# Key pages of a paged decode: products and sums by halves of a page in every stage outside the attentions

## The chip, the cores and the metric

The kernel is one launch on one core of a Trainium2 chip. The core has five engines that run beside each other, each through its own list of instructions in a fixed order: TensorE (PE, matrix products; PEld is its loading of weights), VectorE (DVE), ScalarE (ACT), GpSimd (POOL) and SyncE (SP). An instruction waits on semaphores until what it reads has been written and what it overwrites has been read; what stands behind it on the same engine waits with it. SP, ACT and POOL also issue the DMA transfers. The metric is the time of one execution on the device in microseconds (us); of several executions the median counts.

## The reference

One step of a decoder layer for two groups that share the weights: a prompt of 1024 rows and a sample group of 8 sequences with one new row each. Everything is float32. Cut to what matters here:

```python
def fox_sample(q, k, v, logf, k_pool, v_pool, logf_pool, page_table):      # the 8 samples
    k_all = concatenate([k_pool[page_table].reshape(B, past, H, hd), k])   # past = 64 pages x 128 keys
    v_all = concatenate([v_pool[page_table].reshape(B, past, H, hd), v])
    c = cumsum(concatenate([logf_pool[page_table]..., logf]))
    return fox_attend(q, k_all, v_all, c[:, past:], c, qpos, kpos)

def fox_attend(q, k, v, cq, ck, qpos, kpos):
    s = einsum('bqhd,bkhd->bhqk', q, k) * 64 ** -0.5 + (cq - ck)           # then causal mask
    return einsum('bhqk,bkhd->bqhd', softmax(s), v)

# prompt: input projection -> attention (8 heads of 64) and spatial gating -> output projection
#         -> cross-attention into 256 memory rows (4 heads of 256)
#         -> MLP: up to 2 x 2816 columns, causal convolution of width 3, silu(gate) * val, down
# sample: the same layers, with fox_sample in place of the prompt's attention
```

For each of the 8 samples the scores `s` need 8192 cached keys of 8 heads x 64 numbers, gathered through the page table, multiplied with the sample's query and summed over the 64 numbers of each head.

## The kernel before

**The prompt (main work).** `prompt()` runs it in stages, named in `phase[0]`: `p1` (RMSNorm statistics and the input projection in column blocks Q, F, K, V, Z), `att0` and `att1` (the attention of rows 0 to 511 and 512 to 1023), then for each half of the rows `mid0`/`mid1` (output projection and cross-attention) and `ffn0`/`ffn1` (the MLP). The matrix products take float32 operands split in a high and a low part: `wload` loads a weight tile `wr`, ACT writes the high part `wh` (line 235), DVE the low part `wl` (line 236, `wr - wh`), and `gemm3` issues three products for each pair (lines 272, 273, 274). There are 4 buffers for `wl`. In the MLP, DVE also reads each up-projected tile out of PSUM for the convolution (lines 1299, 1300) and adds the down-projection to the residual (line 1332).

**The samples (background work).** `decode()` reads the cache. The 8192 keys of a sample are spread over the 128 partitions; one *page* below is a tile `kv` of 128 x 2048 numbers (1 MB): 4 keys of 512 numbers in each partition. There are 16 such pages of keys and 16 of values for each sample, 128 and 128 in all. `kstep(b, ch, st)` handles one page of keys: POOL gathers it (line 1420), DVE multiplies it in place with the query `qb` (line 1436), and sums each head's 64 products into the scores `s` (line 1440). After a sample's 16 pages come its softmax (`soft_max`, `soft_all`, `soft_exp`), and then `vstep`: POOL gathers a page of values (line 1482), and PE multiplies it by the weights in 4 narrow products (line 1488), 16 for a pair of pages. Keys and values share a ring of 4 `kv` buffers: POOL can gather the next page only when DVE has summed a page of keys, or PE has read a page of values. When all samples are through, `sample_rest()` takes them through the other layers.

**How a page of keys is cut.** In `att0`/`attx`/`att1` a page is done by quarters (lines 1427 and 1428, not touched here). Elsewhere the number of pieces is `sp`:

```python
sp = KS if phase[0][:3] == "mid" or held[0] else 1     # KS = 2
m = 4 // sp
```

With `sp = 1` the page is one product and one sum (the stages `p1` and `ffn0`). With `sp = 2` (`mid0`, `mid1`) there is a loop over the two products and behind it a loop over the two sums.

**What sets the order.** The main loop advances the background by a step whenever enough of the main work has been written (`PACE`). `kstep` writes under `behind(ENG.DVE)`, so that its instructions come behind what DVE has been given of the main work. The order written is not the order that runs: a scheduler places all instructions of each engine in a list, with a model of how long each one takes, and picks on each engine what is ready by that model. The lists of all engines are fixed when the program is built. A change of one instruction's size can thus move others.

## Time and profile before

| | |
|---|---|
| median of 3 runs | 1792.09 us (1789.83 to 1795.09) |
| the profiled execution | 1796.66 us, its span 1794.9 us |
| PE busy | 1736.6 us, 97% of the span |
| DVE busy | 1399.3 us, 78% |
| ACT busy | 734.4 us, 41% |
| POOL busy | 496.1 us, 28% |
| mean granted TensorE clock | 0.992 |
| DMA | 521.07 MB, mean 290 GB/s |

How to read the views. Times are in us from the start of the span unless marked ns. A row of instructions gives start and duration, engine, line, operation, `out<-in` by the program's tile names, and the shape; "x2" are two in a row, with the time from the first one's start to the last one's end; in brackets stands the idle time of the engine ahead of it and what ended it. The view by stages gives for each stretch of time how long each engine was busy, with the number of instructions in brackets, the granted clock, and the DMA engines' share and rate. Durations of neighbours on an engine can overlap by a little, so that the distance from start to start is the time that an instruction takes from the engine. A row of the waits says which engine and line waited for which, the total, how often, and the longest.

By the first rows of lines 236, 272 and 1332 of each stage, the stages lie about here: `p1` 0 to 260, the attentions 260 to 495, `mid0` 495 to 712, `ffn0` 712 to 1130, `mid1` 1130 to 1345, `ffn1` 1345 to 1780.

### The profile page before, as it was taken

To read this page: it belongs to the slowest core of one execution; us is meant where nothing else is said; L and a number is where in the kernel's file an instruction comes from. 1 tells how busy PE (TensorE), PEld (TensorE's weight loads), DVE (VectorE), ACT (ScalarE), POOL (GpSimd) and SP (SyncE) were. 2 spreads that over 40 slices of the span, in tenths; PEclk is the share of its full clock that TensorE was granted. 3 is DMA by queue.
4 is the path that set the end of the run, shared out by engine and by line. 5 is a ranking of instruction groups with operands and counts; after the bars stand their busy time and mean duration, and the time that the engine had idled before them with its cause. 6 is when DMAs were issued, how large, how long until landed. Compare 5 with 4: busy or idle time off the path is not lost.

```text
span 1794.9 us, 25099 instructions
## 1 busy us (share of the span) xinstructions
PE 1736.6 (97%) x9637; PEld 1286.9 (72%) x9637; DVE 1399.3 (78%) x1733; ACT 734.4 (41%) x1374; POOL 496.1 (28%) x461
## 2 busy tenths in 40 slices
PE   8999999889999999999999999999999999999997
PEld 5887777655677667777777777776676778767875
DVE  4689658988788987999999999887885549855344
ACT  6332256466643635333333244335353233333332
POOL 1252334432222332233322223333322122102110
PEclk9999999999999999999999999999999999999999
DMA  8886888787697975779788878978879687568982
GB/s 299 304 295 222 301 324 318 260 274 230 254 401 279 366 300 222 287 289 349 293 304 311 289 309 318 382 292 331 312 288 343 221 301 250 192 259 299 358 311 81
DMA packets 157075, 521.07 MB, mean 290 GB/s; under 512 B 20874, under 2 KB 40842, under 8 KB 124186
## 3 DMA queue, kind: packets, MB, share of 16 engines
q0 software_dynamic: 57168, 341.14, 50.2%
q1 hardware_dynamic: 92874, 165.73, 26.6%
q10 hardware_dynamic: 6912, 12.59, 1.9%
q8 instruction: 76, 1.25, 0.3%
q14 instruction: 45, 0.37, 0.1%
HBM read 495.47 MB, written 23.93 MB: 289 GB/s over the span
## 4 chain that ended last, share of the span: by engine, by line
PE 53%; DMA 9%; issue 8%; DVE 6%; POOL 2%; ACT 2%; POOLq 0%; DVEq 0%; ACTq 0%; SPq 0%
DMA kv<-cache_v,io 7%; PE ba L272 6%; PE ba L274 6%; PE ba L273 6%; PE dv L1488 4%; PE bb L272 3%; PE bb L273 3%; PE bb L274 3%; PE ba L1065 1%; PE ba L1064 1%; PE ba L1066 1%; PE dv L331 1%; DVE kv L1436 1%; PE dv L1764 1%; DVE s L1440 1%
## 5 line engine op out<-in xcount | busy, mean ns | idle before, releaser
L235 ACT ACTIVATE wh<-wr 128x1024 fp32r<-128x1024 f32 (+2 forms) x220 | 228.7, 1044 | 438.9 <-PE ba L273 152.7
L236 DVE TENSOR_TENSOR wl<-wr,wh 128x1024 fp32r<-128x1024 f32 (+2 forms) x220 | 263.0, 1200 | 165.7 <-PE ba L274 58.0
L1420 POOL DMA_INDIRECT kv<-cache_k,io x128 | 188.8, 1475 | 589.2 <-DVE s L1440 317.7
L1436 DVE TENSOR_TENSOR kv<-kv,d 128x1024 f32<-128x1024 f32 (+1 forms) x156 | 258.0, 1681 | 25.0 <-DMA kv<-cache_k,io 25.0
L1440 DVE TENSOR_REDUCE s<-kv 128x16 f32<-128x1024 f32 (+1 forms) x156 | 258.4, 1673 | 0.0
L1482 POOL DMA_INDIRECT kv<-cache_v,io x128 | 168.7, 1318 | 243.2 <-PE dv L1488 155.6
L272 PE MATMUL ba<-u,wh 128*128 128x512 f32 x528 | 209.8, 398 | 0.0
L273 PE MATMUL ba<-u,wh 128*128 128x512 f32 x528 | 208.8, 395 | 0.5 <-DVE u L239 0.5
L274 PE MATMUL ba<-u,wl 128*128 128x512 f32 x528 | 209.2, 397 | 0.0
L272 PE MATMUL ba<-wh,u 128*128 128x512 f32 (+1 forms) x495 | 186.1, 379 | 0.9 <-ACT u L235 0.9
L273 PE MATMUL ba<-wl,u 128*128 128x512 f32 (+1 forms) x495 | 185.3, 375 | 1.5 <-DVE wl L236 1.5
L274 PE MATMUL ba<-wh,u 128*128 128x512 f32 (+1 forms) x495 | 183.2, 375 | 0.0
L1488 PE MATMUL dv<-kv,s 128*32 128x512 f32 x1024 | 126.5, 600 | 4.6 <-DMA kv<-cache_v,io 4.6
L274 PEld LDWEIGHTS ba<-u,wl 128*128 128x128 f32 x528 | 99.5, 188 | 28.3 <-issue 5.7
L272 PEld LDWEIGHTS ba<-u,wh 128*128 128x128 f32 x528 | 99.6, 189 | 26.6 <-issue 4.8
L273 PEld LDWEIGHTS ba<-u,wh 128*128 128x128 f32 x528 | 99.6, 189 | 25.1 <-issue 2.3
L272 PEld LDWEIGHTS ba<-wh,u 128*128 128x128 f32 x495 | 93.0, 188 | 25.0 <-issue 6.5
L272 PE MATMUL bb<-u,wh 128*128 128x512 f32 x272 | 108.6, 399 | 0.0
L273 PE MATMUL bb<-u,wh 128*128 128x512 f32 x272 | 107.9, 397 | 0.1
L274 PE MATMUL bb<-u,wl 128*128 128x512 f32 x272 | 107.9, 397 | 0.0
L273 PEld LDWEIGHTS ba<-wl,u 128*128 128x128 f32 x495 | 93.1, 188 | 20.7 <-DVE wl L236 2.5
L274 PEld LDWEIGHTS ba<-wh,u 128*128 128x128 f32 x495 | 92.9, 188 | 19.4 <-issue 1.6
(451 smaller groups left out, 3311.9 us busy)
## 6 DMA issues: line engine op xcount, KB each, us to landing
wr<-w_up SPq DMA_DIRECT2D x88, 512.0 KB
kv<-w_up POOLq DMA_DIRECT2D x22, 1024.0 KB
wr<-w_down SPq DMA_DIRECT2D x40, 512.0 KB
kv<-w_down POOLq DMA_DIRECT2D x11, 1024.0 KB
wr<-w_in SPq DMA_DIRECT2D x16, 512.0 KB
wr<-w_o SPq DMA_DIRECT2D x16, 512.0 KB
wr<-w_cq SPq DMA_DIRECT2D x16, 512.0 KB
wr<-w_co SPq DMA_DIRECT2D x16, 512.0 KB
```

The lines of the kernel that those rows point to most:

```text
L235: nc.scalar.activation(h, src, AF.Copy)
L236: nc.vector.tensor_tensor(l, src, h.bitcast(F32), op=ALU.subtract)
L272: mmul(out, sh, mh, start=(i == 0), stop=False)
L273: mmul(out, sh, ml, start=False, stop=False)
L274: mmul(out, sl, mh, start=False, stop=(i == n - 1))
L331: mmul(ps[32 * j : 32 * j + 32, :w], xT[:, k, :] if nk == 8 else xT[:, k * 8 : k * 8 + 32], raw[:, q, j * w : (j + 1) * w], start=(k == 0) ...
L1064: mmul(pss[i], mh[k][:, tb], wh, start=(k == korder[0]), stop=False)
L1420: nc.gpsimd.indirect_dma_start(kv, None, a["cache_k"], off(kidx[:, b, ch : ch + 1]))
L1436: nc.vector.tensor_tensor(kvv[:, i : i + m, :], kvv[:, i : i + m, :], qb.unsqueeze(1).broadcast_to((P, m, 512)), op=ALU.mult)
L1440: nc.vector.tensor_reduce(s[:, ch * 4 + i : ch * 4 + i + m, :].rearrange("p k h -> p (k h)"), kvv[:, i : i + m, :].rearrange("p k (h d) -> ...
L1482: nc.gpsimd.indirect_dma_start(kv, None, a["cache_v"], off(kidx[:, b, ch : ch + 1]))
L1488: mmul(dv[32 * j : 32 * j + 32, :], s[:, ch * 4 : ch * 4 + 4, :].rearrange("p k h -> p (k h)"), kvv[:, j, :], start=(ch == 1), stop=(ch == ...
```

## The change

Outside the attentions `sp` is always `KS = 2`, and the loop header between products and sums is gone, so that each half's sum is written right behind its product:

```diff
-            sp = KS if phase[0][:3] == "mid" or held[0] else 1
+            sp = KS
             m = 4 // sp
             with behind(ENG.DVE):
                 for i in range(0, 4, m):
                     nc.vector.tensor_tensor(
                         kvv[:, i : i + m, :], kvv[:, i : i + m, :], qb.unsqueeze(1).broadcast_to((P, m, 512)), op=ALU.mult
                     )
-                for i in range(0, 4, m):
                     nc.vector.tensor_reduce(
```

In `p1` and `ffn0` a page becomes two products of 128x1024 and two sums instead of one of 128x2048 each; in `mid0` and `mid1` only the written order of the four instructions differs. Lines behind 1437 move up by one, so that the sum of line 1440 is line 1439 afterwards.

What the scheduler makes of it shows on DVE. The first place is the start of the block V of the input projection in `p1`. `wl_203` to `wl_212` are the low parts of V's four weight tiles, for which PE waits; `t2_180` and `dec_165` belong to the samples' gates; `kv_183` and the like are pages of keys. Before:

```order
L545 TENSOR_SCALAR t2_180_1288<-t2_178_1276 8x512
L1436 TENSOR_TENSOR kv_183_1319<-kv_183_1319,d2_61_345 128x2048
L1436 TENSOR_TENSOR kv_190_1382<-kv_190_1382,d2_61_345 128x2048
L1436 TENSOR_TENSOR kv_196_1423<-kv_196_1423,d2_184_1323 128x2048
L1440 TENSOR_REDUCE s_62_347<-kv_183_1319 128x32
L1436 TENSOR_TENSOR kv_200_1460<-kv_200_1460,d2_184_1323 128x2048
L236 TENSOR_TENSOR wl_203_1467<-wr_202_1465,wh_204_1468 128x1024
L1440 TENSOR_REDUCE s_62_347<-kv_190_1382 128x32
L236 TENSOR_TENSOR wl_206_1475<-wr_205_1473,wh_207_1476 128x1024
```

The same place on DVE with the change:

```order
L1436 TENSOR_TENSOR kv_183_1347<-kv_183_1347,d2_61_345 128x1024
L1436 TENSOR_TENSOR kv_190_1412<-kv_190_1412,d2_61_345 128x1024 x2
L1436 TENSOR_TENSOR kv_196_1455<-kv_196_1455,d2_184_1353 128x1024
L1439 TENSOR_REDUCE s_62_347<-kv_183_1347 128x16
L1436 TENSOR_TENSOR kv_196_1455<-kv_196_1455,d2_184_1353 128x1024
L1439 TENSOR_REDUCE s_62_347<-kv_183_1347 128x16
L1439 TENSOR_REDUCE s_62_347<-kv_190_1412 128x16
L1436 TENSOR_TENSOR kv_200_1494<-kv_200_1494,d2_184_1353 128x1024 x2
L236 TENSOR_TENSOR wl_203_1503<-wr_202_1501,wh_204_1504 128x1024
L1439 TENSOR_REDUCE s_62_347<-kv_190_1412 128x16
L236 TENSOR_TENSOR wl_206_1511<-wr_205_1509,wh_207_1512 128x1024
```

Ahead of these rows stand the first half's product of `kv_183` and the `dec` row. Before, four products and one sum of a whole page stand between the gates' rows and `wl_203`; now eight products and three sums of halves (five and a half pages' worth instead of five). No half's sum stands right behind its product.

The second place is DVE in `ffn0`, at the first down-projection: `wl_1393` and `wl_1396` are two of its weight tiles. Before:

```order
L1436 TENSOR_TENSOR kv_1356_6875<-kv_1356_6875,d2_1251_6233 128x2048
L1300 SCALAR_TENSOR_TENSOR t2_1368_6960<-bb_1367_6935,gp_82,t2_1368_6960 128x510
L236 TENSOR_TENSOR wl_1393_7103<-wr_1392_7101,wh_1394_7104 128x1024
L236 TENSOR_TENSOR wl_1396_7109<-wr_1395_7107,wh_1397_7110 128x1024
L1436 TENSOR_TENSOR kv_1369_6965<-kv_1369_6965,d2_1251_6233 128x2048
L236 TENSOR_TENSOR u_1358_6890<-t2_1355_6870,u_1357_6889 128x512
L1440 TENSOR_REDUCE s_1252_6235<-kv_1356_6875 128x32
```

The same place on DVE with the change:

```order
L1436 TENSOR_TENSOR kv_1356_6941<-kv_1356_6941,d2_1251_6285 128x1024 x2
L1300 SCALAR_TENSOR_TENSOR t2_1368_7028<-bb_1367_7003,gp_82,t2_1368_7028 128x510
L236 TENSOR_TENSOR wl_1393_7177<-wr_1392_7175,wh_1394_7178 128x1024
L1436 TENSOR_TENSOR kv_1369_7033<-kv_1369_7033,d2_1251_6285 128x1024 x2
L236 TENSOR_TENSOR wl_1396_7183<-wr_1395_7181,wh_1397_7184 128x1024
L236 TENSOR_TENSOR u_1358_6958<-t2_1355_6936,u_1357_6957 128x512
L1439 TENSOR_REDUCE s_1252_6287<-kv_1356_6941 128x16 x2
```

The page `kv_1369` now stands ahead of `wl_1396` instead of behind it, and both halves of a page are multiplied before either is summed. PE's list is the same before and after from the attention to the start of `ffn0`, and in nearly all of `ffn1`; in the rest of `p1`, in `ffn0` and in `mid1` products move by some places.

## The prediction

> **What bounds the kernel now.** I read the sums by stage first: they say in which stage an engine has room. (`p1` without its first 60 us, the attentions, `mid0`, `ffn0`, `mid1`, `ffn1`; columns: length, then PE, PEld, DVE, ACT, POOL busy.)

> ```profile
> 60.00:230.00 170.00, 168.38 (x954) 133.25 (x950) 142.82 (x108) 55.19 (x78) 55.80 (x31) 1.00 0.77 276
> ...
> 260.00:495.00 235.00, 212.24 (x1376) 149.88 (x1376) 197.43 (x348) 144.94 (x318) 81.72 (x104) 0.98 0.78 266
> 495.00:712.00 217.00, 211.88 (x1069) 157.36 (x1068) 184.48 (x234) 97.27 (x211) 65.87 (x50) 0.99 0.83 319
> 712.00:1130.00 418.00, 416.51 (x1974) 310.41 (x1973) 394.34 (x372) 153.31 (x238) 127.69 (x91) 1.00 0.82 304
> 1130.00:1345.00 215.00, 205.04 (x1025) 147.93 (x1025) 181.94 (x215) 91.19 (x196) 70.32 (x54) 0.98 0.85 320
> 1345.00:1780.00 435.00, 434.07 (x2857) 321.48 (x2857) 248.99 (x368) 143.46 (x252) 68.93 (x96) 1.00 0.72 265
> ```

> PE bounds it. In the two stages where whole pages are cut, PE idles 1.6 us of 170 (`p1`) and 1.5 us of 418 (`ffn0`). So there is next to nothing to win there; what can be won lies in stages whose pages were halves already, above all `mid1` (10 us idle). DVE is the engine that the change loads: it has 27 us of room in that stretch of `p1`, and 23.7 us in `ffn0`, where it is busy for 94%.

> Then the waits of PE, for those two stages apart: the first row is all that PE waited for in `p1` from 60 to 240, the other two all in `ffn0`.

> ```profile
> PE ba L273 <- DVE wl L236: 1.5, 4, 0.7
> ...
> PE dv L1488 <- DMA kv<-cache_v,io: 1.1, 1, 1.1
> PE bb L944 <- DVE u L239: 0.4, 1, 0.4
> ```

> In `p1` PE waits for a `wl` of DVE, in `ffn0` practically for nothing: DVE runs ahead of it there, and the four `wl` buffers hold the lead. A late DVE costs time only where the lead is short.

> **The change, part by part.**

> *Halves instead of whole pages.* By shape, products and sums of the whole run:

> ```profile
> L1436 DVE TENSOR_TENSOR kv<-kv,d 128x2048 f32<-128x2048 f32 x68 | 154.4, 2280 | 12.0 <-DMA kv<-cache_k,io 12.0
> L1440 DVE TENSOR_REDUCE s<-kv 128x32 f32<-128x2048 f32 x68 | 154.1, 2273 | 0.0
> L1440 DVE TENSOR_REDUCE s<-kv 128x16 f32<-128x1024 f32 x88 | 104.3, 1208 | 0.0
> L1436 DVE TENSOR_TENSOR kv<-kv,d 128x1024 f32<-128x1024 f32 x88 | 103.5, 1218 | 13.0 <-DMA kv<-cache_k,io 13.0
> ```

> 68 pages are whole: 26 in `p1`, 42 in `ffn0` (row of each stage further down). By durations two halves cost 2 x 1218 - 2280 = 156 ns more for the product and 2 x 1208 - 2273 = 143 ns for the sum, 0.30 us a page. But neighbours on DVE overlap, so starts tell more. Whole pages, then two products of halves and what follows them, then two sums and what follows them:

> ```profile
> 92.70 2.28 DVE L1436 TENSOR_TENSOR kv<-kv,d 128x2048 f32<-128x2048 f32 x1
> 94.90 2.28 DVE L1440 TENSOR_REDUCE s<-kv 128x32 f32<-128x2048 f32 x1
> 97.10 2.28 DVE L1436 TENSOR_TENSOR kv<-kv,d 128x2048 f32<-128x2048 f32 x1
> ...
> 643.05 2.35 DVE L1436 TENSOR_TENSOR kv<-kv,d 128x1024 f32<-128x1024 f32 x2
> 645.31 1.21 DVE L1440 TENSOR_REDUCE s<-kv 128x16 f32<-128x1024 f32 x1
> ...
> 1147.68 2.33 DVE L1440 TENSOR_REDUCE s<-kv 128x16 f32<-128x1024 f32 x2
> 1149.94 2.35 DVE L1436 TENSOR_TENSOR kv<-kv,d 128x1024 f32<-128x1024 f32 x2
> ```

> Whole: 2.20 us from start to start for either. Two halves: 2.26 us for either. So a page costs DVE 2 x 0.06 = 0.12 us more; this is the value I take, since it is what the engine loses in a row of such instructions, and 0.30 us is the upper end. Over 68 pages that is 8.2 us (at most 20.3), in `ffn0` 42 x 0.12 = 5.0 us (at most 12.6) against 23.7 us of idle DVE.

> [...]

> *Sum right behind the product.* The order shows that it does not happen: the halves' products stand in pairs and the sums behind. In `mid0` DVE's list reads as before, and in `mid1` it differs in where rows stand, not in how a page is done. Worth 0.

> *The V block of `p1`.* Here the lead is nil. DVE, with the rows of the first order piece, and PE at that moment:

> ```profile
> 132.27 0.15 DVE L367 SCALAR_TENSOR_TENSOR lfs<-fs,lse 8x8 f32<-8x8 f32 x1 [4.99 <-ACT lse L366]
> ...
> 138.65 4.47 DVE L1436 TENSOR_TENSOR kv<-kv,d 128x2048 f32<-128x2048 f32 x2
> ...
> 151.77 6.68 DVE L1436 TENSOR_TENSOR kv<-kv,d 128x2048 f32<-128x2048 f32 x3
> 158.38 2.27 DVE L1440 TENSOR_REDUCE s<-kv 128x32 f32<-128x2048 f32 x1
> 160.57 2.27 DVE L1436 TENSOR_TENSOR kv<-kv,d 128x2048 f32<-128x2048 f32 x1
> 162.77 1.21 DVE L236 TENSOR_TENSOR wl<-wr,wh 128x1024 fp32r<-128x1024 f32 x1
> ...
> 164.03 0.50 PE L273 MATMUL ba<-wl,u 128*128 128x512 f32 x1 [0.29 <-DVE wl L236]
> ```

> `wl` ends at 163.98 and PE starts at 164.03, after waiting. From 151.77 to 162.77 are five whole instructions, 11.0 us. With the change eleven halves stand there: 11 x 1.13 = 12.4 us, 1.4 more. What was lost earlier in `p1` is taken up by the 5 us in which DVE waits for ACT at 132; the two pages at 138.65 add 2 x 0.12. So PE starts V 1.7 us later, and the rows of PE ahead of it are the same: **+1.7 us** (0 if ACT or a load is late there anyway, 3.0 with full durations, 11 x 1.218 and 0.6). The next tiles, `wl_206` and `wl_209`, come sooner behind `wl_203` than before, with one half between them instead of a whole page.

> *The Z block of `p1`.* The fourth `wl` now stands behind two pages instead of one.

> ```profile
> 211.00 2.29 DVE L1436 TENSOR_TENSOR kv<-kv,d 128x2048 f32<-128x2048 f32 x1 [1.32 <-DMA kv<-cache_k,io]
> 213.21 1.22 DVE L236 TENSOR_TENSOR wl<-wr,wh 128x1024 fp32r<-128x1024 f32 x1
> ...
> 218.03 0.39 PE L273 MATMUL ba<-wl,u 128*128 128x512 f32 x1
> ```

> It ended at 214.4 and PE first used it at 218.0. From 211.0 there now run two products of halves, another `wl`, two sums, two products, and then this `wl`: 7 x 1.13 + 1.21 = 9.1 us, so it ends at 220.1. PE's list has 16 narrow products more ahead of the use, about 1.9 us (such sixteen take 1.93 us in the row at 781.75 below), so PE wants it at 219.9: **+0.2 us** (0 to +2).

> *The MLP, `ffn0`.* The shortest leads are at the first tiles of a down-projection. This is the second order piece:

> ```profile
> 781.75 1.93 PE L1488 MATMUL dv<-kv,s 128*32 128x512 f32 x16 [1.12 <-DMA kv<-cache_v,io]
> ...
> 786.79 2.29 DVE L1436 TENSOR_TENSOR kv<-kv,d 128x2048 f32<-128x2048 f32 x1 [3.69 <-DMA kv<-cache_k,io]
> 789.66 2.35 DVE L236 TENSOR_TENSOR wl<-wr,wh 128x1024 fp32r<-128x1024 f32 x2
> ...
> 797.12 0.39 PE L273 MATMUL ba<-wl,u 128*128 128x512 f32 x1
> ```

> The second `wl` ended at 792.0, PE used it at 797.1: a lead of 5.1 us. With a page's two products (2.26 us) ahead of it, 2.8 us are left. DVE's own 5.0 us spread over 418 and fall into idle time such as the 3.7 us here. I take **+0.3 us**, one wait as small as the 0.4 us of `L944`; ends 0 and +5.0, the whole extra unhidden. The page itself is given back at most 2 x 0.12 us later, so POOL's gather of the next one moves little.

> *`mid1`.* Its pages cost the same; its rows stand differently because `ffn0` ends differently. I take 0, with ends of -5 and +5, half of its 10 us of idle PE either way.

> Sum: 1.7 + 0.2 + 0.3 = **+2.2 us**. Against the profiled execution that is 1796.66 + 2.2 = 1798.9 us; it lies 4.6 us above the median of the runs, so against the median I predict 1792.1 + 2.2 = **1794.3 us**, 0.12% more. About 0.3% (5.4 us) is what a measurement of this kernel can tell from no change.

> **The rivals.**

> *Values come late (slower).* In `ffn0` PE takes a pair of pages of values every 20 us or so, and POOL gets buffers when DVE has summed or PE has read:

> ```profile
> PE dv L1488 <- DMA kv<-cache_v,io: 4.6, 3, 3.3
> ...
> POOL kv L1420 <- DVE s L1440: 123.7, 24, 10.7
> POOL kv L1420 <- PE dv L1488: 98.0, 14, 13.6
> ...
> 712.00:1130.00 418.00, 95.77 (x42) 1.00 0.82 304
> ```

> (First row: whole run; the next two `ffn0`; the last: the 42 products of `ffn0`, 95.77 us.) Products with values stand up to 80 rows later in PE's new list, behind a sample's softmax, so pairs pile up. For: the longest such wait is already 3.3 us. Against: only three in the whole run. If three more of the 21 pairs (x336 narrow products) wait for 3 us each, the time is 1794.3 + 9 = 1803 us. It decides once a page's sum comes later than the lead of its pair. A DVE bound in `ffn0` belongs here: at full durations, 394.3 + 12.6 = 407 of 418 us leaves 11, still no bound; all 12.6 on PE would give 1806.

> *Shorter blocks let `mid1` run better (faster).* A half holds DVE for 1.2 us instead of 2.3, and `mid1`'s list is a new one. If it saves 6 of the 10 us that PE idles there, and the V block costs nothing: 1792 - 6 = 1786 us; with the V block 1788. For: 3.3 us idle at each of two turns. Against: its pages were halves before.

> *The change does nothing.* For the order within a page it is so, by the lists, and it is in the sum; the halving does take place.

> **How the numbers follow.** The forecast, within 2 to 3 us of 1794.3: 0.52, all within 0.3% (its own range 1790 to 1797). Values late or DVE too full: 0.32, slower by over 0.3%. `mid1` better: 0.16, faster by over 0.3%. The range reaches from the better `mid1` (1786) to DVE's whole extra on PE (1807), leaving out about one in six.

> **What would show it.** In the profile after: no 128x2048 products, 156 + 68 = 224 halves in the row of each line, DVE's total up by 8 to 20 us; PE's wait for `wl` in `p1` up by 1 to 3 us and V's start later; PE idle in `ffn0` still under 4 us. Wrong if PE shows waits of more than 5 us in `ffn0` for `cache_v` or `wl`, or if `mid1` is shorter or longer by more than 5 us, or if time moves in the attentions, whose lists are the same.

## The result and the profile after

The changed kernel takes 1805.21 us (median of five; 1803.29 to 1809.74) against 1792.09 us of the kernel before (median of five; 1789.73 to 1795.09): a ratio of 1.0063, 95% interval 1.0042 to 1.0084. By this ratio it is 11.3 us more, with an interval of about 7.5 to 15 us; the medians themselves are 13.1 us apart. Two executions further down, one of `turn_free` (1939.26 us at a granted clock of 0.845) and one of `all_whole` (2147.85 us at 0.751), were slow and are left out of the medians and ratios. The prediction, 1794.3 us, had called "no change" the likeliest; the time fell into its range, where its slower rival lay. The two profiled executions, 1796.66 and 1805.21 us, are 8.5 us apart, and it is these 8.5 us that the traces can explain.

By shape, products and sums of the whole run after the change (lines behind 1437 have moved up by one, so the sum is L1439, the products with values L1487):

```profile
L1439 DVE TENSOR_REDUCE s<-kv 128x16 f32<-128x1024 f32 x224 | 264.7, 1205 | 0.0
L1436 DVE TENSOR_TENSOR kv<-kv,d 128x1024 f32<-128x1024 f32 x224 | 262.8, 1215 | 30.5 <-DMA kv<-cache_k,io 30.2
```

All 224 are halves, and DVE's busy time has gone from 1399.3 to 1407.1 us: 7.8 us, where the starts had given 8.2. The change loads DVE as was worked out; the question is where PE pays for it. The stages (length, PE, PEld, DVE, ACT, POOL busy):

```profile
60.00:230.00 170.00, 165.48 (x932) 132.05 (x928) 143.66 (x152) 53.54 (x75) 44.01 (x29) 0.99 0.75 266
...
712.00:1130.00 418.00, 413.61 (x1968) 308.29 (x1968) 394.27 (x450) 151.35 (x238) 123.08 (x86) 1.00 0.80 297
1130.00:1345.00 215.00, 204.68 (x1022) 147.66 (x1021) 185.68 (x217) 89.53 (x191) 76.45 (x59) 0.98 0.87 334
```

PE idles 4.5 us in that stretch of `p1` (before 1.6) and 4.4 us in `ffn0` (before 1.5); `mid1` is as it was. The waits of PE, the first two rows of the whole run, the others between 1075 and 1125 us:

```profile
PE ba L273 <- DVE wl L236: 4.1, 4, 2.9
PE dv L1487 <- DMA kv<-cache_v,io: 2.8, 2, 1.9
...
PE ba L944 <- DMA t<-sgn_d: 2.0, 1, 2.0
PE ba L944 <- DMA u<-an_d: 1.5, 1, 1.5
```

So two places carry it. The wait for `wl` in `p1` is 2.6 us longer, and at the turn from `ffn0` to `mid1`, where the merge's transposes (L944) begin, PE waits 3.5 us for loads that were there in time before (`sgn_d` and `an_d` are results of the gating and of the attention, kept in DRAM, which the merge reads back). Waits for values have become less, 2.8 us instead of 4.6.

*The V block.* DVE and PE in the changed kernel:

```profile
134.49 0.48 DVE L527 MEMSET t<- 8x512 f32 x1 [3.32 <-DMA o_k<-t]
...
140.20 4.61 DVE L1436 TENSOR_TENSOR kv<-kv,d 128x1024 f32<-128x1024 f32 x4
...
154.69 4.61 DVE L1436 TENSOR_TENSOR kv<-kv,d 128x1024 f32<-128x1024 f32 x4
...
166.02 1.21 DVE L236 TENSOR_TENSOR wl<-wr,wh 128x1024 fp32r<-128x1024 f32 x1
...
167.28 0.66 PE L273 MATMUL ba<-wl,u 128*128 128x512 f32 x1 [2.88 <-DVE wl L236]
...
...
170.72 0.47 PE L272 MATMUL ba<-wh,u 128*128 128x512 f32 x1
171.03 0.39 PE L273 MATMUL ba<-wl,u 128*128 128x512 f32 x1
```

`wl` starts at 166.02 instead of 162.77, and the first product behind it at 167.28 instead of 164.03. Of these 3.25 us the halves in the block make the 1.4 that were worked out; the other 1.8 DVE brings along. It comes to the two pages at 140.20 instead of 138.65, and loses another 0.24 on them. Its idle time at 132 does not take up what was lost ahead: in this order a MEMSET (L527) stands there that waits until the store of `o_k` has read the tile. All seven traces with halves in `p1` have this wait (3.2 to 7.8 us) and come to the two pages at 138.97 to 140.76 us; the seven with whole pages there don't have it and come at 137.03 to 138.65.

The wait is not all: the eight products behind it take 0.63 us and stand 0.43 us apart (from 167.28 to 170.72 in eight steps), then they are back at 0.39 us and 0.23 us apart. Eight times 0.2 us is another 1.6 us. The views by short stretches show why (the number ahead of the last two is the granted clock):

```profile
167.20:171.20 4.00, 3.92 (x10) 3.10 (x11) 4.00 (x5) 0.19 (x1) 1.69 (x1) 0.57 0.74 204
171.20:175.20 4.00, 4.00 (x18) 3.22 (x18) 4.00 (x5) 0.88 (x1) 0.92 (x1) 1.00 1.00 392
```

After 2.9 us without work PE was granted 0.57 of its clock in the mean of 4 us; the trace has it at half from 167.46 to 170.87, for 3.41 us, and at full again behind that.

*The turn.* PE, POOL and SP in the changed kernel:

```profile
1103.83 0.33 PE L944 MATMUL ba<-cp,t 128*128 128x128 f32 x1 [1.98 <-DMA t<-sgn_d]
...
1089.44 0.94 POOL L1420 DMA_INDIRECT kv<-cache_k,io  x1 [14.44 <-PE dv L1487]
...
1094.21 0.94 POOL L1420 DMA_INDIRECT kv<-cache_k,io  x1 [0.34 <-DVE s L1439]
...
1095.28 0.32 SPq L986 DMA_DIRECT2D t<-sgn_d  x1
```

Three of the four transposes run at 1100.20 us; the fourth waits for a load that SP issued at 1095.28, right behind four pages of 1 MB that POOL issued within 5 us (the first and the last are shown) after a wait of 14.4 us. Two explanations offer themselves: the pages hold up the load, or DVE is late (it frees the `t` buffer that the load goes into). The experiments decide between them.

### The profile page after: what moved, and what is told of

It reads as the page before. It is cut to its first block, busy times and chain, and to the rows that moved or that the text cites. A ratio compares the mean times of both kernels' runs of the same rounds, so it can differ in the third digit from the quotient of the medians.

```text
span 1803.4 us, 25237 instructions
## 1 busy us (share of the span) xinstructions
PE 1739.9 (96%) x9637; PEld 1289.8 (72%) x9637; DVE 1407.1 (78%) x1869; ACT 732.8 (41%) x1374; POOL 483.6 (27%) x461
## 4 chain that ended last, share of the span: by engine, by line
PE 65%; DVE 7%; DMA 4%; issue 3%; ACT 2%; POOL 1%; DVEq 0%; POOLq 0%; SPq 0%; ACTq 0%
PE ba L272 8%; PE ba L274 8%; PE ba L273 8%; PE dv L1487 5%; PE bb L272 4%; PE bb L274 4%; PE bb L273 4%; DVE kv L1436 1%; PE ba L1064 1%; PE ba L1066 1%; PE ba L1065 1%; PE dv L331 1%; PE dv L1763 1%; DVE s L1439 1%; DVE wl L236 1%
## 5 line engine op out<-in xcount | busy, mean ns | idle before, releaser
L236 DVE TENSOR_TENSOR wl<-wr,wh 128x1024 fp32r<-128x1024 f32 (+2 forms) x220 | 262.7, 1198 | 170.6 <-PE ba L274 60.4
L1420 POOL DMA_INDIRECT kv<-cache_k,io x128 | 181.4, 1417 | 604.1 <-DVE s L1439 316.6
L1436 DVE TENSOR_TENSOR kv<-kv,d 128x1024 f32<-128x1024 f32 x224 | 262.8, 1215 | 30.5 <-DMA kv<-cache_k,io 30.2
L1439 DVE TENSOR_REDUCE s<-kv 128x16 f32<-128x1024 f32 x224 | 264.7, 1205 | 0.0
L273 PE MATMUL ba<-u,wh 128*128 128x512 f32 x528 | 209.0, 396 | 0.0
L273 PE MATMUL ba<-wl,u 128*128 128x512 f32 (+1 forms) x495 | 185.7, 377 | 4.1 <-DVE wl L236 4.1
L1487 PE MATMUL dv<-kv,s 128*32 128x512 f32 x1024 | 126.0, 598 | 2.8 <-DMA kv<-cache_v,io 2.8
L273 PEld LDWEIGHTS ba<-u,wh 128*128 128x128 f32 x528 | 99.6, 189 | 26.2 <-issue 4.1
L273 PEld LDWEIGHTS ba<-wl,u 128*128 128x128 f32 x495 | 93.7, 189 | 22.0 <-DVE wl L236 5.1
L273 PE MATMUL bb<-u,wh 128*128 128x512 f32 x272 | 107.6, 396 | 0.0
```

The lines of the kernel that those rows point to most:

```text
L236: nc.vector.tensor_tensor(l, src, h.bitcast(F32), op=ALU.subtract)
L273: mmul(out, sh, ml, start=False, stop=False)
L1420: nc.gpsimd.indirect_dma_start(kv, None, a["cache_k"], off(kidx[:, b, ch : ch + 1]))
L1436: nc.vector.tensor_tensor(kvv[:, i : i + m, :], kvv[:, i : i + m, :], qb.unsqueeze(1).broadcast_to((P, m, 512)), op=ALU.mult)
L1439: nc.vector.tensor_reduce(s[:, ch * 4 + i : ch * 4 + i + m, :].rearrange("p k h -> p (k h)"), kvv[:, i : i + m, :].rearrange("p k (h d) -> ...
L1487: mmul(dv[32 * j : 32 * j + 32, :], s[:, ch * 4 : ch * 4 + 4, :].rearrange("p k h -> p (k h)"), kvv[:, j, :], start=(ch == 1), stop=(ch == ...
```

## The experiments

How PE's time shifts is read in all of them in one way: the start of each matrix product is compared with that of the same product (line and tile) in the profile before, and the median difference is taken in stretches of 20 us of the time before. Where the lists are the same but for the edit, a step in this row is a loss at that place. The table is of one execution each, and it can lie off its kernel's median: that of `ffn0_halves` is 6.0 us above it, those of `both_moved`, `ffn0_quarters`, `sgn_early` and `before_turn_free` are 3.6 to 5.0 us below. It shows places; what a version costs is taken from the medians and ratios.

| offset to before, us, at | 140 | 200 | 480 | 700 | 1040 | 1120 | 1300 | 1400 |
|---|---|---|---|---|---|---|---|---|
| the changed kernel | 0.7 | 4.8 | 5.3 | 5.7 | 5.3 | 8.9 | 6.7 | 8.5 |
| `p1_halves` | 0.0 | 3.7 | 2.9 | 3.9 | 4.6 | 3.9 | 2.4 | 1.6 |
| `ffn0_halves` | 0.1 | -0.4 | -1.3 | 2.8 | 3.1 | 9.7 | 10.8 | 10.4 |
| `v_first` | 0.2 | -0.2 | -2.1 | 5.0 | 5.5 | 9.8 | 15.4 | 14.7 |
| `merge_first` | 0.1 | 4.4 | 3.3 | 9.6 | 9.6 | 17.4 | 12.5 | 13.0 |
| `sgn_early` | 1.3 | 5.7 | 5.5 | 7.4 | 7.1 | 11.6 | 10.8 | 10.5 |
| `turn_free` | 0.6 | 5.0 | 3.2 | 4.0 | 4.1 | 2.3 | -2.2 | 2.6 |
| `both_moved` | 0.5 | 0.8 | -2.2 | 4.2 | 4.6 | 2.1 | -4.0 | 0.6 |
| `ffn0_quarters` | 0.2 | -0.3 | -3.3 | -3.6 | 0.7 | 9.4 | 8.2 | 5.5 |
| `all_whole` | -0.3 | -0.6 | -0.5 | 0.6 | 1.5 | 2.4 | 3.9 | 5.5 |
| `mid1_whole` | 0.2 | -0.4 | -2.3 | 1.2 | 1.8 | 1.7 | 3.6 | 2.0 |
| `before_v_first` | 0.3 | 0.1 | 1.3 | 1.4 | 1.7 | 2.1 | -0.8 | -2.0 |
| `before_turn_free` | -0.1 | -0.7 | -4.0 | -4.0 | -3.8 | -5.7 | -11.9 | -8.7 |

One warning belongs to the table. `ffn0_halves`, `mid1_whole`, `ffn0_quarters` and `before_turn_free` have the list of before up to the start of `ffn0`, and yet they stand at 2.8, 1.2, -3.6 and -4.0 us at 700: one list varies by several us from run to run, around 400 and 610 us (from 480 to 700 us the changed kernel loses 0.4 us, and `merge_first` with the same list there 6.3). Only steps that come back are used.

Theory A: the time goes where a wait arises, and nowhere else. Theory B: every page by halves costs the same, as DVE's load. Theory C: the list is another one, and another list comes out longer or shorter by luck. Theory D, formed later, says what is late at the turn. That the two loops have become one needs no run: the changed kernel comes out as the same program with one loop and with two, instruction by instruction on all five engines, and so does the kernel before.

### Halves in one stage alone

```diff
-            sp = KS
+            sp = KS if phase[0] != "ffn0" or held[0] else 1
```

> Pages by halves in p1 and mid, whole pages in ffn0 as before; the lists of all engines are those of the changed kernel up to the start of ffn0. Theory A (place): the time is lost where a wait is, at the V block (first products with wl some 4 us later than before, 2.6 of it more waiting and 1.6 of it products at half speed behind the wait) and not by DVE's load: +1 us at 60 us, +4 at the V block, +5 to +6 us by the start of ffn0, and no step at 1084 to 1100, so 1797 to 1798 us, +5 to +6 against before. Theory B (load): every page by halves costs the same, wherever it is: 26 of the 68 pages, 26/68 x 11.3 = +4.3 us, which rises evenly over p1. Theory C (the list as a whole is a matter of luck): a time anywhere from -5 to +10, with no step at the V block.

```diff
-            sp = KS
+            sp = KS if phase[0] != "p1" or held[0] else 1
```

> Whole pages in p1 as before, halves in ffn0 and mid; the lists are those of before up to the start of ffn0. Theory A (place): nothing up to 1050 us although DVE does 5 us more in ffn0, then what the changed kernel lost at the turn from ffn0 to mid1 and to ffn1, net +2.5 to +3 us: 1795 us. Theory B (load): 42/68 x 11.3 = +7.0 us, 1799 us, growing evenly over ffn0. Theory C: the turns depend on the list of the moment and come out otherwise than in the changed kernel, -3 to +3 us.

Halves in `p1`: ratio 1.0023 (1.0004 to 1.0041), 1800.4 us. Halves in `ffn0`: 1.0026 (1.0009 to 1.0044), 1801.05 us. Together 0.49%, 8.8 of the 11.3 us. The time alone does not tell A from B (4.1 and 4.7 us against B's 4.3 and 7.0), the place does. With halves in `p1` the offset is 0.0 at 140 us and 3.7 at 200, all of it at the V block; the turn costs nothing (4.6, then 3.9). With halves in `ffn0` it is the other way round: nothing at the V block, 2.8 at 700 us and 3.1 at 1040, where B would have grown by most of its 7, and 9.7 at 1120. PE's wait at the V block in the first, at the turn in the second, and the clock behind the second:

```profile
PE ba L273 <- DVE wl L236: 2.4, 1, 2.4
```

```profile
PE ba L944 <- DMA t<-sgn_d: 3.6, 1, 3.6
...
1103.90:1107.90 4.00, 3.98 (x10) 3.21 (x11) 0.81 (x2) 0.69 (x1) 0.00 (x0) 0.50 1.04 394
1107.90:1112.00 4.10, 4.10 (x22) 1.47 (x22) 4.05 (x4) 0.72 (x2) 0.94 (x1) 0.75 1.01 390
```

Behind the wait of 2.4 us the clock was at half for 3.4 us (0.64 in the mean of 166.1 to 170.1), as in the changed kernel. A holds as to the places, and B falls. That `ffn0_halves` loses 6.6 us at the turn and the changed kernel 3.6, with the same list there, has a reason in the second fence: its one wait was 3.6 us instead of two of 2.0 and 1.5, and behind it the clock was at half for 6.8 us, which is 3.4 us of PE's time; behind the other two it stayed at full, as the changed kernel's row shows:

```profile
1103.80:1107.80 4.00, 3.97 (x22) 2.42 (x26) 2.93 (x4) 0.99 (x2) 0.45 (x1) 1.00 1.07 398
```

By medians `ffn0_halves` is 4.7 us over before, where 2.5 to 3 were expected.

### The page ahead of the V block's first `wl`

The changed kernel, with one page given out a product later:

```diff
-                yield 5.2
+                yield 0.0 if (c0 == O_K and tt == 7) else 10.4 if (c0 == O_V and tt == 0) else 5.2
```

> The changed kernel, with the one page that stands directly ahead of the first wl of the V block moved behind the four wl (its two products of halves, 2.3 us of DVE). Theory A: wl ends 2.3 us sooner, PE's wait there falls from 2.9 to about 0.5 us and the slow products behind it go with it: V starts 3.5 to 4 us sooner against the changed kernel, offset against before after the V block +1, the time about 1801 us. If only the wait counts and the slow products come from something else, 2.3 to 2.6 us sooner. Theory B: no more than 0.3 us. What comes after p1 has another list, so the whole time is good to 3 us only; the offset behind the V block decides.

```profile
162.51 1.20 DVE L236 TENSOR_TENSOR wl<-wr,wh 128x1024 fp32r<-128x1024 f32 x1
...
163.77 0.49 PE L273 MATMUL ba<-wl,u 128*128 128x512 f32 x1
```

`wl` comes at 162.51, PE starts V at 163.77 without a wait and at full speed (a granted clock of 1.00 from 164 to 168), and the offset behind the block is -0.2 instead of 4.8 us. So moving 2.3 us of DVE's work was worth 3.5 us by `wl` and 5.0 us behind the block (4.5, if the offsets ahead are taken off), with the 1.6 us of slow products among them. Of the 3.5 us, 2.3 are the page that was moved; by the remaining 1.2 DVE was ahead in this run anyway. The whole time, though, is 1813.76 us, a ratio of 1.01 (1.0077 to 1.0122): the new list behind `p1` loses 7.1 us in `mid0` (where one list alone varied by nearly as much), 5.6 in `mid1` and, like the changed kernel, some 4 at the turn (4.3). For the V block theory A is shown; as for what a new list does elsewhere, C has its first point.

### What is late at the turn

The loads of `w_o` queued on SP behind those of the merge:

```diff
-        nc.sync.dma_start(raw, src)
+        with tc.issue_after(hold[0]) if hold else nullcontext(): nc.sync.dma_start(raw, src)
```

> The changed kernel, with the loads of w_o in mid1 queued on SP behind the merge's loads of sgn_d and an_d; all else up to there is the same. Theory A (SP's order makes the step at 1084 to 1100): PE's waits for sgn_d and an_d at L944 (2.0 and 1.5 us) go, the step of +3.3 us there falls to under 1, and the time to about 1802 us. Rival: the t buffers that sgn_d is loaded into come free too late anyway (DVE is late), and the step stays: 1805 us. If the w_o loads are now what is late, a wait for wl of w_o takes the place: 1804 to 1808 us.

```profile
PE bb L272 <- ACT u L235: 3.0, 1, 3.0
PE ba L944 <- DMA t<-sgn_d: 1.4, 1, 1.4
```

1807.66 us, 1.0056 (1.0037 to 1.0076). The wait for `sgn_d` is shorter, but another of 3.0 us has taken its place, and the step is 7.8 instead of 3.6 us: 4.4 us of waiting, and 3.4 for a clock at half from 1109.84 to 1116.67. What PE now waits for is not a `wl` of `w_o`, as the expectation's last case had it, but `u`, the split of the MLP's own last tile. SP's order alone is not the cause.

Then the load itself moved ahead of two of the four pages (the third tile gets another buffer, and the fourth one's load is issued at 1092.57):

```diff
-            t = T2()
+            t = turns_() if hf and i == 2 else T2()
```

> The changed kernel, with the third of the merge's four sgn_d tiles loaded into the xg tile, free since mid0, so that the fourth takes the t buffer of the third and its load stands on SP at about 1089.6 us, ahead of three of the four loads of pages that POOL issues from 1089.4 to 1094.2 us, instead of at 1095.3 behind all four. Theory A (pages stand ahead of the merge's load in the DMA engines): the 2.0 us wait at L944 for sgn_d goes, the step at 1084 to 1100 us falls from +3.3 to +1 or less, the time to about 1803 us, as far as mid1's new list allows. Rival 1 (DVE is late there, whatever the loads): PE stops for a product of DVE in the same place and the step stays +3. Rival 2 (the wait comes from the w_o loads): nothing changes, 1805 us.

```profile
1105.69 0.69 DVE L1306 TENSOR_TENSOR t<-t,t 128x512 f32<-128x512 f32 x1
...
1106.41 0.63 ACT L235 ACTIVATE u<-t 128x512 fp32r<-128x512 f32 x1 [1.15 <-DVE t L1306]
...
1107.10 0.50 PE L272 MATMUL bb<-wh,u 128*128 128x512 f32 x1 [2.69 <-ACT u L235]
```

The wait for `sgn_d` is gone, and 2.7 us of waiting for that same `u` stand in its place, at a step of 4.5 us. ACT waits for L1306, DVE's last product of the MLP. This is the expectation's rival 1: DVE is late, whatever the loads. The changed kernel has it too, hidden behind the load: ACT's split is done at 1104.10 us, and PE takes it at 1104.15, so that it would have stood until then with the load in time:

```profile
1103.47 0.63 ACT L235 ACTIVATE u<-t 128x512 fp32r<-128x512 f32 x1 [0.76 <-DVE t L1306]
...
1104.15 0.51 PE L272 MATMUL bb<-wh,u 128*128 128x512 f32 x1
```

The time of `sgn_early`, 1811.47 us and 1.0099 (1.008 to 1.0118), is worse again, with 3.7 us of waiting for a `wl` in `mid1`'s new list.

How late DVE is in the changed kernel, its products at L1306 show. First before, and then after, the one of two tiles earlier and the last one:

```profile
1074.19 0.67 DVE L1306 TENSOR_TENSOR t<-t,t 128x512 f32<-128x512 f32 x1
...
1093.18 0.68 DVE L1306 TENSOR_TENSOR t<-t,t 128x512 f32<-128x512 f32 x1
```

```profile
1080.83 0.67 DVE L1306 TENSOR_TENSOR t<-t,t 128x512 f32<-128x512 f32 x1
...
1102.77 0.67 DVE L1306 TENSOR_TENSOR t<-t,t 128x512 f32<-128x512 f32 x1
```

The last is 9.6 us later than before, 4.3 more than the offset of 5.3 that PE has there, and 2.9 of these arise in this stretch: 19.0 us from one to the other before, 21.9 after, with DVE busy practically all the time in both. Between them stood four whole instructions of pages (4 x 2.20 = 8.8 us), and now stand ten halves (10 x 1.13 = 11.3) and another sample's small reduction (L1476, 1.1 us): not 0.12 us a page, but a product of a whole page that the new list sets ahead of the last tiles instead of behind them. So the two pages there were moved as a last test, theory D:

```diff
-                hc2 = []
+                hc2 = []; held[0] = held[0] or bool(late) and f >= NF - 2
...
-                side = late()
+                side = late(); held[0] = False
```

> The changed kernel, with the two pages whose products and sums stand ahead of the last four tiles of ffn0's MLP (about 9 us of DVE) given out some 20 us later, behind those tiles. Theory D (DVE is what is late at the turn from ffn0 to mid1; the load of sgn_d and the split u, which ended its wait in the kernel without that load, both follow from DVE's last products L1306): with that work gone L1306 ends some 4 us sooner, PE's waits for sgn_d and u there vanish, the step at 1084 to 1100 us falls from +3.3 to below +1. Rival (each is late for itself, the loads by the DMA engines): a wait of 2 us or more for a load stays at L944. The V block's step of +4 stays. The whole time 1798 to 1803 us, if mid1's new list costs nothing.

```profile
PE dv L1488 <- DMA kv<-cache_v,io: 0.7, 1, 0.7
```

```profile
PE ba L280 <- ACT u L238: 4.8, 2, 4.6
```

The first row is all that PE waits for between 1075 and 1125 us; the second is from its waits between 1130 and 1380 us. At the turn the waits for `sgn_d`, `an_d` and `u` are all gone, and the step of +3.6 has become -1.8 (about a pair of value products, 1.9 us, now stands behind the turn). So the turn's loss comes from the two pages, as D has it. This run alone does not tell D from its rival, loads late for themselves, since the pages' gathers moved too: POOL issues one page between 1075 and 1102 us here, where the changed kernel issued four between 1089 and 1095. That DVE alone suffices, `merge_first`, `sgn_early` and the row at 1104.15 show; whether the load would be late by itself stays open. The V block's 4.4 us remain. The time is 1802.54 us (median of five), at the upper end of the 1798 to 1803 expected, and the ratio 1.0053 (1.0037 to 1.0069): 0.1% under the changed kernel's, which the intervals don't resolve. A new wait at the turn to `ffn1` (the second row, `L280`, 4.6 us for `u`) took some 4 us back.

### Both moves, and DVE loaded more

> Both moves at once: the page ahead of the V block's first wl, and the two pages ahead of ffn0's last tiles, still by halves everywhere. Theory A and D: offset against before after the V block under +0.5, at the turn no more step, so at the start of mid1 +1 to +2 beside what mid0 varies by from run to run (0 to +4), and the whole change costs 0 to 4 us: 1794 to 1799 us. Theory C (any list other than that of before loses a few us at turns that nobody named): slower again by 5 us or more, with waits in mid1.

```profile
PE ba L273 <- DVE wl L236: 0.6, 1, 0.6
...
PE bb L1116 <- DVE u L1016: 3.9, 1, 3.9
```

With both edits the V block costs 0.3 us and the turn nothing; in `mid1` it is even ahead of before. The median is 1802.29 us, 1.0042 (1.0028 to 1.0055), above the 1794 to 1799 us expected: two thirds of the loss against before are left (0.42 of 0.63%). The trace does not show where: its execution, 1798.42 us, is the fastest of the six and ends only 1.8 us behind the profiled one of before, with a 3.9 us wait at the turn to `ffn1`. The granted clock makes little of it, 0.992 in the mean of the six and 0.993 in the eleven of before beside them. The named places are healed as A and D say, but the time is that of C. This is not settled further.

Quarters in `ffn0`, whole pages in `p1`:

```diff
-            sp = KS
+            sp = KS if phase[0][:3] == "mid" or held[0] else 4 if phase[0] == "ffn0" else 1
```

> As the kernel with halves in ffn0 alone, but by quarters: by starts (two quarters 1.28 us, three 1.86) a page costs DVE 0.36 us more than whole, 42 x 0.36 = 15 us in ffn0, three times the halves' 5. Theory A and D: up to 1060 us the offset stays under +3, as PE has its wl early, and the lateness shows at the turn, where DVE's last products come later: a step of +4 to +12 there; 1800 to 1806 us. Theory B (load): it grows evenly over ffn0, by 3 x 5 = 15 us, 1809 us. If neither grows over ffn0 nor the step at the turn is larger than with halves, the load of DVE plays no part and the step is the list's.

```profile
1060.00:1130.00 70.00, 65.23 (x307) 47.93 (x306) 65.78 (x107) 31.20 (x55) 23.99 (x13) 0.95 0.83 297
```

```profile
PE ba L944 <- DMA t<-sgn_d: 2.5, 1, 2.5
...
PE bb L272 <- ACT u L235: 1.8, 2, 1.4
...
PE ba L944 <- DVE t L1300: 0.5, 1, 0.5
```

1805.97 us, 1.0065 (1.0053 to 1.0078), within A's and D's 1800 to 1806; B's 1809 is not far off, but the place speaks against it. Over `ffn0` up to 1040 the offset rises by 4.3 us (more than the 3 expected), at the turn by 8.7 in one step: 4.8 us of waits (2.5 for `sgn_d`, 1.8 for `u`, 0.5 for a `t` of L1300) and a clock of 0.95 over 70 us, which is 3.5 us. Three times the extra load on DVE makes 4.8 us of waits at the turn, where halves made 3.5 and 3.6.

### The other direction, and a faster version

Whole pages in `mid0` and `mid1` as well, and in `mid1` alone (kernel before, `sp = 1`, and `sp = KS if phase[0] == "mid0" else 1`):

> The kernel before, with the 44 pages of mid0 and mid1 whole as well: DVE does 44 x 0.12 = 5.3 us less. Theory A (place): nothing up to the start of mid0, and then a whole product of 2.2 us in front of a wl or a split of the mixing and crossing adds a wait of 1 to 2 us at one or two turns: 1795 to 1800 us. Theory B (load): 44 x 0.17 us (11.3 us over 68 pages) = 7.3 us less, 1788 us, from the median of before in its own run. Theory C (the list): -5 to +10 us, without a link to the length of a product.

> The kernel before, with the 23 pages of mid1 alone whole, the lists those of before up to the start of mid1: DVE does 2.8 us less there. Theory A (place): whether mid1 is longer or shorter is set by its waits; 0 to +4 us. Theory B (load): -3.9 us. Theory C (the list): anything from -5 to +10 us, with waits of other kinds than before has in mid1.

1800.74 us, 1.0042 (1.0024 to 1.0061), and 1797.94 us, 1.0022 (1.0006 to 1.0038). DVE does less in both, and both are slower: B is wrong in its sign. In `mid1`, where before waited 3.3 us, the products with values wait 4.7 and 4.3 us for their page:

```profile
PE dv L1488 <- DMA kv<-cache_v,io: 4.7, 1, 4.7
```

```profile
PE dv L1488 <- DMA kv<-cache_v,io: 4.3, 1, 4.3
```

> The kernel before, with the whole page ahead of the V block's first wl moved behind the four wl. Theory A: PE's wait there (0.3 us) goes and V starts 0.3 to 0.5 us sooner, nothing more, as without slow products there is nothing else to win; the rest of the time by the list that follows, -3 to +5 us. If V starts more than 1 us sooner, something else than wl is late in before.

1795.31 us, 1.001 (0.9993 to 1.0027): no difference. V starts without its wait of 0.3 us, and there was nothing else to win, as expected.

Last, the two pages moved from ahead of the turn in the kernel before (the edit of `turn_free` on whole pages):

> The kernel before, whole pages as they were, with the two pages given out behind ffn0's last tiles as in the changed kernel's trial. In that trial mid1 came out 4.5 us shorter against before (offset 2.3 to -2.2 us between 1080 and 1300), as the 3.3 us wait for a page of values in mid1 was gone, and the turn to ffn1 4.0 us longer. Theory A and D: nothing at the turn to mid1 (there is only a 0.4 us wait to win), -3 to -5 us in mid1, and if the wait at the turn to ffn1 (4.6 us for u at L280) does not come along, 1788 to 1790 us against 1792 to 1796 of before; if it does, the same time as before. Theory C: slower by 2 us or more, as nearly every list but the one of before has been.

1793.74 us against 1796.95 of before in the same runs: 0.998, 95% interval 0.9964 to 0.9995. It is the one version here that is faster than both kernels, by 0.2% of the one before, some 3 us (about 1 to 6); as it is one of twelve that were tried, and its interval ends just below 1, this is weak evidence. From 1040 us, ahead of which its list is that of before, the offset goes from -3.8 to -5.7 at the turn, -11.9 in `mid1` and -8.7 in `ffn1`: 4.9 us won from the edit on in this execution, which is 5.0 us under its median. Of the 6.2 us in `mid1` up to 3.4 are the clock's: before has two stretches of 3.4 us at half there, from 1178.61 and 1250.29 us, this one none. A wait for values of 4.2 us stays and stands late, at the turn to `ffn1`, where 3.2 us are lost again.

## Why the prediction was right and wrong

- **The extra on DVE** (0.12 us a page, 8.2 us in all) was right: 7.8 us. The durations would have given 20.3.
- **The order within a page** (worth 0) was right: the lists are the same with one loop and with two.
- **The V block of `p1`** ("PE starts V 1.7 us later") was the right place and mechanism, mis-sized. The eleven halves took what was worked out (from 154.69 to 166.02 are ten halves, 11.33 us, 1.133 each, for 1.13). But `wl` came 3.25 us later and not 1.7, and PE's wait out at 2.4 to 2.9 us in the runs with this list, where 0.3 + 1.7 = 2.0 was expected. The term put at nothing was what DVE had lost earlier in `p1`: the wait at 132 was to take it up, but in the new order that wait ends with the store of `o_k`, and 1.55 us came through. And a term was missing altogether: behind this wait PE's clock was at half for 3.4 us, which cost another 1.4 to 1.6 us. The offset behind the block came to 3.7 to 4.4 us more than ahead of it instead of 1.7.
- **The Z block** (+0.2 us) was right: the offset is 4.8 us at 200 and 4.9 at 260.
- **The MLP, `ffn0`** (+0.3 us, "DVE's own 5.0 us ... fall into idle time") is the step that failed. For 330 of its 418 us it held: the offset is 5.7 at 700 and 5.3 at 1040. The failure is at the end of the stage, whose leads the prediction did not work out: the MLP's last split hangs on DVE's last L1306 and the merge's last load on the one before it, DVE has no idle time there, and the new list put a page's product ahead of them. It cost 3.6 us here and 6.6 in `ffn0_halves`, waits of 3.5 and 3.6 us. The leads that were worked out are those of `wl` tiles at the first down-projection.
- **`mid1`** (0, with 5 us either way) was within its bounds: -2.2 us from 1120 to 1300, and +1.8 at the turn to `ffn1`.
- **The sum** was 2.2 us; the two mis-sized terms make 4.1 + 3.6 = 7.7 of the 8.5 us between the profiled executions. What is left, 0.8 us, is less than one list varies by.
- **The rivals.** "Values come late" named 1803 us and was near by time, but by luck, not by its mechanism: waits for values fell to 2.8 us. Its second half, a DVE too full in `ffn0`, had the engine right and the form wrong: no bound over the stage, but one stretch at its end. "`mid1` better" had no net effect in the changed kernel; in `before_turn_free` it was real.
- **What would show it** came in as written for the halves and the wait for `wl` (up 2.6 us, where 1 to 3 was written), and nearly so for DVE's total (up 7.8, where 8 to 20 was written). PE idles 4.4 us in `ffn0`, just over the 4 us, and no single wait was over 5 us.

What stays open: why the kernel with both places healed still measures 0.42% more than before. In the changed kernel part of the loss may be the clock's beyond the V block: its five executions had 0.989 in the mean, those of before in the later runs 0.992 to 0.993, and the time at half rate that this stands for would be some 6 us more, by estimate and at the most, as PE does not lose by it where it waits anyway. Eleven of the twelve other lists tried here are not faster than that of before, ten of them slower, also those in which DVE does less; that would fit losses at turns that each list has in its own way, but no run took those apart.

## What to carry to other kernels

An engine's idle time in a stage is no room for more work if it lies in another part of the stage than the work: look at the last instructions of a stage for which the next one waits, and count what the new order sets ahead of them. A wait of TensorE has to be priced with the clock behind it, which here made 2.4 us of waiting into 3.8, 2.9 into 4.5 and 3.6 into 6.6, but added nothing to two waits of 2.0 and 1.5. And a change that only moves a list's order has to be judged by steps that come back in several kernels, as one list alone varied by some 3 us at one place and 6 at another. An experiment that moves work should be read for everything that moves with it: two pages taken from DVE's list took their gathers along.

## What the hardware showed unexpectedly

```profile
164.05:167.46 3.41, 0.53 (x2) 0.22 (x3) 3.41 (x4) 0.00 (x0) 0.00 (x0) 1.00 0.81 276
167.46:170.87 3.41, 3.41 (x9) 2.63 (x10) 3.41 (x4) 0.00 (x0) 1.69 (x1) 0.50 0.73 198
```

```profile
1247.61:1251.03 3.42, 2.01 (x8) 0.88 (x6) 3.42 (x5) 1.96 (x7) 0.94 (x1) 1.00 1.00 395
1251.03:1254.44 3.41, 1.84 (x16) 0.42 (x16) 2.06 (x3) 1.44 (x6) 0.47 (x1) 1.00 1.05 422
1254.44:1257.85 3.41, 3.16 (x22) 2.68 (x19) 0.20 (x2) 2.46 (x7) 2.37 (x3) 1.00 0.73 212
```

In the first, PE is busy for 0.53 us of a step, and the next step is at half. In the second the wait is longer, but it falls into two steps with 2.01 and 1.84 us of work, and the clock stays at full. In the traces of before and of the changed kernel, from 60 to 1775 us, the steps at full clock with one at half behind them had at most 1.89 us of work (the one from 409.80 in the changed kernel), and those with one at full behind them at least 1.53 (the one from 1252.90 there); between these both occur. At the V block of `p1_halves` a gap of 2.4 us, of which 1.9 us fell into one step, had a step at half behind it.

So the same list in the same place can cost differently. At the turn from `ffn0` to `mid1` the waits and the slow stretches behind them add up to the steps: waits of 3.5 and 4.4 us and no slow stretch to 3.6 (the changed kernel) and 4.3 (`v_first`), 2.7 us and one to 4.5 (`sgn_early`), 3.6, 4.4 and 4.8 us and two to 6.6, 7.8 and 8.7 (`ffn0_halves`, `merge_first`, `ffn0_quarters`). And from 360 to 430 us, with the same list, the clock was 0.93 in before and 1.00 in `before_turn_free`, which gained 3.3 us from 200 to 480.

*The same list, another time.* In `mid0` the issue of one gather on POOL took 1.68 us before and 5.09 us in `mid1_whole`, which has the same list there; PE's wait for `t` a little later was 1.45 us in the one and 3.56 in the other:

```profile
604.30 1.68 POOL L1420 DMA_INDIRECT kv<-cache_k,io  x1 [0.51 <-DVE s L1440]
...
619.54 2.64 PE L1180 MATMUL ba<-t,u 128*128 128x256 f32 x11 [1.45 <-ACT t L1167]
```

```profile
602.03 5.09 POOL L1420 DMA_INDIRECT kv<-cache_k,io  x1 [0.52 <-DVE s L1440]
...
619.38 3.06 PE L1180 MATMUL ba<-t,u 128*128 128x256 f32 x8 [3.56 <-ACT t L1167]
```

The offset of `mid1_whole` goes from -2.3 to 1.2 us there, with a slow stretch of the clock of 3.4 us behind the longer wait. That the late gather is what PE came to wait for fits the rows (the gather's page is DVE's, and DVE's next result is ACT's), but was not tested.
